# Layer 2's pooled gate from seven block products per pair of tiles, with sums of weights made by DMA

## The chip, the cores and the metric

The kernel runs on one core of a Trainium2 chip. The metric is the device time of one execution, in microseconds; lower is better.

## What is computed

A residual stream of 528 tokens (16 learned ones ahead of 512) and 1024 features goes through two layers. The parts that matter here:

```python
h = rmsnorm(x)                                   # x * rsqrt(mean(x*x) + eps) * gain
u_pool, z_pool, c_q, c_kv, k_rope, z_mla, g_pool, g_mla = split(h @ w_in)
y_pool = (pool_mix(u_pool) * silu(z_pool)) @ pool_w_up
y_mla  = (attention(c_q, c_kv, k_rope) * silu(z_mla)) @ mla_w_up
x = x + (sigmoid(g_pool) * y_pool + sigmoid(g_mla) * y_mla) @ w_out
```

Attention is causal, with 8 heads, and normalises queries and keys. g_pool and g_mla are 1024 features wide each. Only the last 512 tokens of the second layer are put out.

## The kernel before

**Numbers and tiles.** Features lie on the 128 partitions, tokens run along the row. Every fp32 product is made of three matmuls of a faster 32-bit type: activations x and weights w are split into a rounded part and the rest (xh + xl, wh + wl), and mm3 (L184 to L187) accumulates wh*xh, wh*xl and wl*xh in PSUM. Activations of the normalised stream are hs: eight pairs hh, hl of 128 features each. hs holds x times the gain, without the norm's factor inv; what reads a product of hs multiplies by inv (tile rinv) when it empties PSUM. The lines are those of before, which the profile of before carries; in the changed kernel the same lines stand further down.

**The stream.** Weights are read once, in chunks of 128x512 (256 KB). SP loads a chunk into one of three buffers raw; ScalarE rounds it to whi (L180), VectorE subtracts to get wlo (L181), three buffers each. A list called plan holds the products (Gemm) in order: an output tile of 128 features is one Gemm of one or two chunks, whose eviction (evac) runs when its last chunk is through. In layer 1 (the second of two, counted from 0) a tile covers 512 tokens, so a chunk is 12 matmuls of 512 columns and a tile of 1024 inputs is 24. The generator stream() puts out two k steps at a time; clk adds up their planned time. The names in layer 1's plan: pu (pooled path up, into xb), zm (attention's silu gate), gp (pooled gate, eight tiles gp0 to gp7), gm (attention's gate, eight tiles), mu (attention up), o (output).

**Order of the work.** go() writes a layer out. Attention's steps are put between pieces of the stream: fill and gap advance the stream by a planned time (FILL, one number per layer), fill_now by a given one, upto to the end of a named product, after() postpones a function until clk has gone on. A scheduler then settles the order on each engine, and behind() adds a wait on another instruction by hand. qk_stats makes nqs (L685), the negative scale of each query, by Newton steps on VectorE. head() multiplies scores into PSUM tiles S (three banks), finds row maxima on VectorE with nqs (L730), takes exponentials on ScalarE (L737), the reciprocal of their sums on VectorE (L769), and normalises on GpSimd (L774, L776). pv() transposes the result on TensorE (L796), splits it, and multiplies by the values (L801, L802) into one PSUM bank o. Other products use four PSUM banks mm.

**Evictions the change touches.** ev_silu empties zm with two operations on VectorE and one on ScalarE (L505 to L508). ev_gp empties a tile of gp: VectorE multiplies by inv (L573), ScalarE takes tanh, VectorE multiplies into xb (L575). ev_gm: VectorE multiplies by inv (L873), ScalarE takes tanh (L874), and the gate stays in SBUF until ev_mu (L882) reads it. ev_pu writes xb (L567). ev_o adds the residual, loaded from DRAM scratch (scr), and stores (L898). In layer 1, scr holds the stream that came out of layer 0.

## Time and profile before

| | us |
|---|---|
| median of 3 runs | 790.47 (789.48 to 790.82) |
| span of the profiled execution | 787.1 |
| median less that span | 3.4 |
| TensorE busy in it | 780.9 |
| VectorE busy | 535.1 |
| ScalarE busy | 410.8 |
| GpSimd busy | 194.4 |

The profiled execution's own time is its span; what lies around it (start and end of the launch) is the third row, by the median. Engines: PE is TensorE, PEld its weight loads, DVE VectorE, ACT ScalarE, POOL GpSimd, SP the queue that issues most transfers. A row of the time line gives start, duration, engine, line, operation, the tile written and those read, shapes, and in brackets the idle time ahead of it with what ended it. Busy times of engines beside TensorE add up work that lies next to it.

### The profile page before, as it was taken

What the parts mean: (1) busy time and instruction counts of PE and PEld (TensorE: products, weight loads), DVE (VectorE), ACT (ScalarE), POOL (GpSimd) and SP (SyncE); (2) the same over time, 40 slices, a digit from 0 to 9 for tenths busy, and PEclk for the clock granted to TensorE, in tenths of its full rate; (3) what the DMA queues carried; (4) which work ended last, traced back from release to release, by engine and by line L of the source; (5) the groups of instructions that cost most, each with busy time, mean ns of one, the idle gap of its engine ahead of it and who ended that gap; (6) DMA issues with size and microseconds to landing.
All of it is one profiled execution on the core that took longest, in us unless ns stands there. A gap on an engine that the chain in (4) does not pass through costs nothing.

```text
span 787.1 us, 14567 instructions
## 1 busy us (share of the span) xinstructions
PE 780.9 (99%) x5301; PEld 708.6 (90%) x5301; DVE 535.1 (68%) x1165; ACT 410.8 (52%) x930; POOL 194.4 (25%) x259
## 2 busy tenths in 40 slices
PE   9999999999999999999999999999999999999998
PEld 8999899999999999999997898887788888887887
DVE  5848787446779987675464487775467888755932
ACT  7645655635656565633354356455445666554420
POOL 1034504002333242051000145131022333410500
PEclk9999999999999999999999999999999999999999
DMA  6242333423223212224642422334232222122372
GB/s 242 82 102 85 96 120 102 128 81 94 96 76 92 78 58 78 95 81 146 192 123 94 95 88 90 129 88 136 96 105 88 95 84 82 65 81 67 102 242 84
DMA packets 52263, 81.83 MB, mean 104 GB/s; under 512 B 8784, under 2 KB 17360, under 8 KB 52192
## 3 DMA queue, kind: packets, MB, share of 16 engines
q1 hardware_dynamic: 52048, 80.65, 32.9%
q8 instruction: 41, 0.67, 0.4%
q14 instruction: 30, 0.25, 0.1%
q10 hardware_dynamic: 144, 0.26, 0.1%
HBM read 74.49 MB, written 4.27 MB: 100 GB/s over the span
## 4 chain that ended last, share of the span: by engine, by line
PE 95%; DMA 2%; DVE 1%; issue 1%; ACT 0%; SPq 0%; ACTq 0%
PE mm L185 28%; PE mm L187 28%; PE mm L186 28%; PE mm L796 2%; PE S L186 2%; PE S L187 1%; PE S L185 1%; PE o L802 1%; PE o L801 1%; PE S L453 1%; DMA xb<-xT 1%; PE mm L355 1%; DVE wlo L181 1%; PE mm L412 0%; DMA rinv<-win 0%
## 5 line engine op out<-in xcount | busy, mean ns | idle before, releaser
L185 PE MATMUL mm<-hh,whi 128*128 128x264 f32 (+2 forms) x1096 | 346.7, 318 | 0.2 <-ACT racc L810 0.2
L186 PE MATMUL mm<-hl,whi 128*128 128x264 f32 (+2 forms) x1096 | 343.9, 315 | 0.0
L187 PE MATMUL mm<-hh,wlo 128*128 128x264 f32 (+2 forms) x1096 | 343.0, 315 | 0.0
L181 DVE TENSOR_TENSOR wlo<-raw,whi 128x512 fp32r<-128x512 f32 (+2 forms) x251 | 188.6, 755 | 119.6 <-ACT whi L180 115.9
L180 ACT ACTIVATE whi<-raw 128x512 fp32r<-128x512 f32 (+2 forms) x251 | 150.4, 601 | 187.5 <-PE mm L186 126.5
L185 PEld LDWEIGHTS mm<-hh,whi 128*128 128x128 f32 x1096 | 205.9, 188 | 13.6 <-ACT racc L810 0.5
L186 PEld LDWEIGHTS mm<-hl,whi 128*128 128x128 f32 x1096 | 206.6, 189 | 11.8
L187 PEld LDWEIGHTS mm<-hh,wlo 128*128 128x128 f32 x1096 | 205.5, 188 | 12.0
L774 POOL TENSOR_TENSOR pm<-pa,rs 128x16 f32<-128x16 f32 x32 | 11.6, 361 | 181.3 <-DVE rs L769 181.3
L560 POOL TENSOR_TENSOR racc<-racc,tmp 128x264 f32<-128x264 f32 (+1 forms) x15 | 14.2, 948 | 153.8 <-ACT tmp L559 129.8
L702 POOL TENSOR_TENSOR tmp<-kp,bc 64x528 f32<-64x528 f32 x16 | 22.5, 1408 | 76.9 <-PE mm L675 44.5
L884 POOL TENSOR_TENSOR tmp<-tmp,xb 128x264 f32<-128x264 f32 (+1 forms) x24 | 27.1, 1149 | 58.2 <-DVE tmp L882 33.1
L730 DVE CUSTOM_DVE_ANT_0 S<-S,maskw,nqs 128x272 f32<-128x272 f32 (+4 forms) x80 | 38.5, 498 | 4.2 <-PE S L187 3.9
L737 ACT ACTIVATE cq<-S,bia 128x400 f32<-128x400 f32 (+2 forms) x48 | 24.6, 516 | 22.6 <-DVE bia L764 12.0
L185 PE MATMUL mm<-u,whi 128*128 128x264 f32 (+1 forms) x108 | 35.2, 326 | 0.0
L187 PE MATMUL mm<-cq,wlo 128*128 128x264 f32 (+1 forms) x108 | 34.5, 323 | 0.7 <-DVE wlo L181 0.7
L187 PE MATMUL mm<-u,wlo 128*128 128x264 f32 (+1 forms) x108 | 34.8, 323 | 0.0
L185 PE MATMUL mm<-cq,whi 128*128 128x264 f32 (+1 forms) x108 | 34.6, 320 | 0.0
L186 PE MATMUL mm<-cq,whi 128*128 128x264 f32 (+1 forms) x108 | 34.5, 321 | 0.0
L277 DVE TENSOR_TENSOR tl<-mm,th 128x512 fp32r<-128x512 f32 (+1 forms) x64 | 29.3, 481 | 6.1 <-ACT th L276 5.1
L776 POOL TENSOR_TENSOR cq<-cq,rs 128x384 f32<-128x384 f32 (+1 forms) x32 | 32.8, 1025 | 0.0
L186 PE MATMUL mm<-kn,whi 128*128 128x264 f32 (+1 forms) x96 | 30.7, 321 | 0.0
(252 smaller groups left out, 1362.4 us busy)
## 6 DMA issues: line engine op xcount, KB each, us to landing
raw<-win SPq DMA_DIRECT2D x143, 256.0 KB, 2.6
raw<-wout SPq DMA_DIRECT2D x32, 256.0 KB, 2.7
bc<-kdr SPq DMA_DIRECT2D x16, 264.0 KB, 3.6
raw<-wpu SPq DMA_DIRECT2D x16, 256.0 KB, 2.7
raw<-wmu SPq DMA_DIRECT2D x16, 256.0 KB, 2.5
raw<-wqb SPq DMA_DIRECT2D x12, 256.0 KB, 2.6
tmp<-xT SPq DMA_DIRECT2D x16, 132.0 KB, 3.0
tmp<-scr SPq DMA_DIRECT2D x7, 256.0 KB, 3.4
```

The lines of the kernel that those rows point to most:

```text
L180: act.activation(hi[:, :n], raw[:, :n], AF.Copy)
L181: dve.tensor_sub(lo[:, :n], raw[:, :n], hi[:, :n].bitcast(F32))
L185: pe.matmul(out, wh, xh, start=start, stop=False)
L186: pe.matmul(out, wh, xl, start=False, stop=False)
L187: newest[0] = pe.matmul(out, wl, xh, start=False, stop=stop)
L277: dve.tensor_sub(lo[:, a:b], src, hi[:, a:b].bitcast(F32))
L702: gp.tensor_mul(kf[r0:r0 + 64, :], self.kp[r0:r0 + 64, :], bc[r0:r0 + 64, :])
L730: dve.tensor_tensor_reduce(out=sv, in0=sv, in1=mask, scale=nqs[:, i, h:h + 1], scalar=3e38, op0=ALU.add, op1=ALU.min, accum_out=bia[:, c:c ...
L737: act.activation(pv, sv, AF.Exp, scale=-1.0, bias=bia[:, i:i + 1], accum_out=rs[:, c:c + 1])
L776: gp.tensor_mul(pt[i][:, NM:], pt[i][:, NM:], rs[:, i:i + 1].to_broadcast([P, n - NM]))
L796: pe.transpose(tr[:, P * (i - j):P * (i - j + 1)], pt[i][:, NM + P * j:NM + P * (j + 1)], ident)
L884: gp.tensor_add(t[:, :b - a], t[:, :b - a], self.am[m][:, a:b])
```

## The change

**Seven products.** For a pair of gp tiles (2u and 2u + 1), the weights are split in two by output tile and in two by input features, the activations in two by input features and in two by tokens (256 each). A 2x2 product of blocks takes eight block products; fast() takes seven, on sums and differences of blocks, and puts the results together afterwards. A block product is one chunk of weights: 12 matmuls of 256 columns, so a pair is 84, where before it was 48 of 512. The products 1, 2 and 4 use a quarter of the weights as they are, the others a sum from DRAM (wsum). PSUM holds a pair in four banks: 1 and 2 in a, 6 in b, 7 and 4 in c, 5 and 3 in d. ScalarE and VectorE (copy, sub, add of 256 columns) join them; got_gp takes tanh and multiplies into xb. The plan's order is now gm0 gm1 gp0 gm2 gp1 gm3 gp2 gm4 gp3 gm5 gm6 gm7, where gp0 to gp3 are the pairs; before it was gp0 to gp7, then gm0 to gm7.

**Sums of weights.** Four per pair, 16 in all. Each is a copy from DRAM to DRAM (256 KB, on SP) and a DRAM-to-DRAM transfer that adds to it (on GpSimd's queue), postponed one by one by SPACE = 4500 of planned time from the start of layer 0's heads. Each waits for a matmul that lies 9000 or 4000 of planned time back.

**Normalised activations.** In layer 1, during qk_stats, renorm() makes hs again with inv in it (four of the eight from xb, four loaded from scr): eight multiplies and eight splits. mixed() makes the differences of activation blocks and splits them, in pieces between the heads' steps. zm and gm then need no inv: ev_zm and ev_gate begin with tanh on ScalarE, straight from PSUM.

**Room.** gm0 to gm5 are stored to DRAM (gate) and loaded again after gm6, because SBUF holds the new blocks meanwhile; the tables for rotary positions share two buffers with them. FILL of layer 1 goes from 2850 to 2700, and flush() at the heads' end, which ran everything postponed, becomes ready(), which runs what is due within 12000. A matmul of head 0's scores in each layer waits for the newest one of the stream.

```diff
-FILL = (2950.0, 2850.0)
+FILL = (2950.0, 2700.0)
...
+SPACE = 4500.0
...
-    def mm3(out, wh, wl, xh, xl, start, stop):
-        pe.matmul(out, wh, xh, start=start, stop=False)
-        pe.matmul(out, wh, xl, start=False, stop=False)
-        newest[0] = pe.matmul(out, wl, xh, start=False, stop=stop)
+    def mm3(out, wh, wl, xh, xl, start, stop, more=False, hold=False):
+        first = pe.matmul(out, wh, xh, start=start, stop=False, skip_group_check=more)
+        if hold:
+            behind(first, newest[0])
+        pe.matmul(out, wh, xl, start=False, stop=False, skip_group_check=more)
+        newest[0] = pe.matmul(out, wl, xh, start=False, stop=stop, skip_group_check=more)
+        past.append((clk[0], newest[0]))
+
+    past = []
+
+    def earlier(ns):
+        return next((m for c, m in reversed(past) if c <= clk[0] - ns), past[0][1])
...
+    def ready():
+        while pend and pend[0][0] <= clk[0] + 12000.0:
+            pend.pop(0)[1]()
...
+    wsum = [dp.tile([P, 4, 512], F32, name=f"wsum{u}") for u in range(4)]
+    gate = dp.tile([P, 6, SEQ], F32, name="gate")
...
+    N2 = SEQ // 2
+    XH = [(NM, NM + N2), (NM + N2, T)]
+    (a, b), (_, c) = XH
+
+    def weight_sums(w):
+        def made(u, i):
+            a, b = w[2 * u], w[2 * u + 1]
+            d = wsum[u]
+            src = {0: (b[:, 0:512], b[:, 512:1024]), 2: (a[:, 0:512], b[:, 0:512]), 1: (a[:, 0:512], d[:, 0, :]),
+                   3: (a[:, 512:1024], d[:, 1, :])}
+            return d[:, i, :], src[i]
+
+        def copy(d, src):
+            behind(sp.dma_start(d, src[0]), earlier(9000))
+
+        def add(d, src):
+            behind(gp.dma_start(d, src[1], accum_op=ALU.add), earlier(4000))
+
+        for u in range(4):
+            for fn, i in ((copy, 0), (copy, 2), (add, 0), (copy, 1), (add, 2), (add, 1), (copy, 3), (add, 3)):
+                yield lambda fn=fn, u=u, i=i: fn(*made(u, i))
...
+        def ev_zm(self, m):
+            def ev(ps, a, b):
+                if a == self.x0:
+                    self.zms[m] = slot(f"u{m}")
+                t = tmp()
+                act.activation(t[:, :b - a], ps, AF.Tanh, scale=0.5)
+                dve.scalar_tensor_tensor(out=self.zms[m][:, a:b], in0=t[:, :b - a], scalar=1.0, in1=ps,
+                                         op0=ALU.add, op1=ALU.mult)
+            return ev
+
+        def renorm(self, k):
+            assert k < 4 or (self.l, f"pu{k}") not in done
+            f = self.f[k] = slot("sv", bufs=2) if k % 4 == 3 else slot(f"cq{k}")
+            f, (hh, hl), x = f[:, NM:T], self.hs[k], xb[:, k, NM:T]
+            if k < 4:
+                sp.dma_start(f, scr[:, k, :])
+                x = f
+            behind(dve.scalar_tensor_tensor(out=f, in0=x, scalar=self.g(G_H + k), in1=self.inv[:, NM:T],
+                                            op0=ALU.mult, op1=ALU.mult), newest[0])
+            split(hh, hl, f, NM, T)
...
+        def mixed(self, i):
+            k, s = divmod(i, 2)
+            if k > 3 or not self.last:
+                return
+            u, w = self.f[k], self.f[k + 4]
+            if s == 0:
+                dve.tensor_sub(w[:, b:c], u[:, b:c], w[:, b:c])
+                dve.tensor_sub(u[:, b:c], u[:, a:b], u[:, b:c])
+                dve.tensor_sub(u[:, a:b], u[:, a:b], w[:, b:c])
+                dve.tensor_sub(w[:, a:b], w[:, a:b], u[:, a:b])
+                return
+            if k == 0:
+                self.half = [sqt().bitcast(F32R) for _ in range(14)]
+                spare = slot("rinv", F32R)
+                self.half += [spare[:, 0:HALF], spare[:, HALF:T]]
+            th, tl = (slot(f"cq{(3, 0, 1, 2)[k] + j}", F32R) for j in (0, 4))
+            t3h, t3l, t4h, t4l = (t[:, :N2] for t in self.half[4 * k:4 * k + 4])
+            split(th, tl, u[:, a:c], a, c)
+            for h_, l_, v in ((t3h, t3l, w[:, b:c]), (t4h, t4l, w[:, a:b])):
+                split(h_, l_, v, 0, N2)
+            self.tt[k] = {6: (th[:, a:b], tl[:, a:b]), 5: (th[:, b:c], tl[:, b:c]), 7: (t3h, t3l), 4: (t4h, t4l)}
+
+        def fast(self, name, a, b, u, got):
+            order = (1, 6, 7, 5, 2, 4, 3)
+            s = wsum[u]
+            src = {1: a[:, 0:512], 2: a[:, 512:1024], 4: b[:, 512:1024], 5: s[:, 0, :], 6: s[:, 1, :], 7: s[:, 2, :],
+                   3: s[:, 3, :]}
+            bank = {}
+
+            def body(i, w):
+                p = order[i]
+                key = {1: "a", 2: "a", 6: "b", 7: "c", 4: "c", 5: "d", 3: "d"}[p]
+                if key not in bank:
+                    bank[key] = mmt()
+                ps = bank[key][:, :N2]
+                t, o = (XH[1] if p == 3 else XH[0]), (0 if p == 1 else 4)
+                for k in range(4):
+                    xh, xl = (x[:, t[0]:t[1]] for x in self.hs[k + o]) if p < 4 else self.tt[k][p]
+                    c = P * k
+                    mm3(ps, w[0][:, c:c + P], w[1][:, c:c + P], xh, xl, k == 0 and p not in (2, 4, 3), k == 3, True)
+                    if k == 1:
+                        yield 6 * (N2 / 2.4)
+                if p == 1:
+                    self.part[u] = slot("sv", bufs=2)
+                d, v = self.part[u][:, 0:N2], self.part[u][:, HALF:HALF + N2]
+                if p == 1:
+                    act.activation(d, ps, AF.Copy)
+                elif p == 6:
+                    dve.tensor_sub(d, d, ps)
+                elif p == 7:
+                    dve.tensor_sub(v, ps, d)
+                elif p == 5:
+                    dve.tensor_sub(v, v, ps)
+                    got(2 * u + 1, XH[1], v, v)
+                elif p == 2:
+                    got(2 * u, XH[0], ps, tmp()[:, :N2])
+                elif p == 4:
+                    x = tmp()[:, :N2]
+                    dve.tensor_sub(x, ps, d)
+                    got(2 * u + 1, XH[0], x, x)
+                else:
+                    dve.tensor_add(d, d, ps)
+                    got(2 * u, XH[1], d, d)
+                if i == len(order) - 1:
+                    done.add((self.l, name))
+                yield 6 * (N2 / 2.4)
+
+            plan.append(Gemm((self.l, name), [src[p] for p in order], 512 * len(order), body=body))
...
+        def got_gp(self, m, s, v, t):
+            am = self.am[m][:, s[0]:s[1]]
+            act.activation(t, v, AF.Tanh, scale=0.5)
+            dve.scalar_tensor_tensor(out=am, in0=t, scalar=1.0, in1=am, op0=ALU.add, op1=ALU.mult)
...
-            fill_now(9500)
+            if self.last:
+                start = clk[0]
+                for i, k in enumerate((4, 5, 6, 7, 0, 1, 2, 3)):
+                    self.renorm(k)
+                    fill_to(start + 1500 * (i + 1))
+            else:
+                fill_now(9500)
...
+                    hold=hold and i == 1)
...
+            between()
...
+        def ev_gate(self, m):
+            def ev(ps, a, b):
+                self.gms[m] = slot(f"cq{m}" if m > 5 else "ts" if m % 2 else "tc")
+                act.activation(self.gms[m][:, a:b], ps, AF.Tanh, scale=0.5)
+                if m < 6:
+                    act.dma_start(gate[:, m, :], self.gms[m][:, a:b])
+            return ev
+
+        def gates_again(self):
+            for m in range(6):
+                self.gms[m] = slot(f"cq{m}")
+                sp.dma_start(self.gms[m][:, NM:T], gate[:, m, :])
...
-                add(f"zm{m}", wi(MT_ZM + m), D, evac=self.ev_silu(self.zms, "u", m), xs=hs, segs=XS)
-            for m in range(8):
-                add(f"gp{m}", wi(MT_GP + m), D, evac=self.ev_gp(m), xs=hs, segs=XS)
-            for m in range(8):
-                add(f"gm{m}", wi(MT_GM + m), D, evac=self.ev_gm(m), xs=hs, segs=XS)
+                add(f"zm{m}", wi(MT_ZM + m), D, evac=self.ev_zm(m) if self.last else self.ev_silu(self.zms, "u", m),
+                    xs=hs, segs=XS)
+            if self.last:
+                for e in ("gm0", "gm1", "gp0", "gm2", "gp1", "gm3", "gp2", "gm4", "gp3", "gm5", "gm6", "gm7"):
+                    m = int(e[2])
+                    if e[:2] == "gp":
+                        self.fast(e, wi(MT_GP + 2 * m), wi(MT_GP + 2 * m + 1), m, self.got_gp)
+                    else:
+                        add(e, wi(MT_GM + m), D, evac=self.ev_gate(m), xs=hs, segs=XS)
+            else:
+                for m in range(8):
+                    add(f"gp{m}", wi(MT_GP + m), D, evac=self.ev_gp(m), xs=hs, segs=XS)
+                for m in range(8):
+                    add(f"gm{m}", wi(MT_GM + m), D, evac=self.ev_gm(m), xs=hs, segs=XS)
...
-            fill_now(2600)
+            if l == 0:
+                fill_now(2600)
+                for i, fn in enumerate(weight_sums([win[1, MT_GP + m] for m in range(8)])):
+                    after(SPACE * (i + 1), fn)
             kq = self.prep(0)
             fill_now(2600)
             due[0] = None
             prev = None
             for h in range(H):
-                kn_ = self.head(h, kq, prev)
+                kn_ = self.head(h, kq, prev, lambda: self.mixed(next(mix)))
                 self.gap()
+                self.mixed(next(mix))
                 if h + 1 < H:
                     kq = self.prep(h + 1)
                 self.pv(prev, (2, 3))
                 prev = kn_
                 self.gap()
+                self.mixed(next(mix))
             fill_now(1300)
             self.pv(prev, (0, 1))
             fill_now(2600)
             if not self.last:
                 self.meta_queries()
             self.pv(prev, (2, 3))
+            up("gm6")
+            if self.last:
+                self.gates_again()
             up("gm7")
-            flush()
+            ready()
```

**On TensorE**, where the pooled gate is made. Before, six rows of tile gp1 (a PSUM tile mm, rounded and rest of hs, weights whi and wlo):

```order
L185 MATMUL mm_7893<-hh_14_133,whi_7889 128x512
L186 MATMUL mm_7893<-hl_15_134,whi_7889 128x512
L187 MATMUL mm_7893<-hh_14_133,wlo_7890 128x512
L185 MATMUL mm_7893<-hh_16_135,whi_7889 128x512
L186 MATMUL mm_7893<-hl_17_136,whi_7889 128x512
L187 MATMUL mm_7893<-hh_16_135,wlo_7890 128x512
```

After, six rows of a product on the differences (sq holds them), then two of a product on hs itself:

```order
L188 MATMUL mm_8215<-sq_7738,whi_8151 128x256
L191 MATMUL mm_8215<-sq_7739,whi_8151 128x256
L192 MATMUL mm_8215<-sq_7738,wlo_8152 128x256
L188 MATMUL mm_8215<-sq_7742,whi_8151 128x256
L191 MATMUL mm_8215<-sq_7743,whi_8151 128x256
L192 MATMUL mm_8215<-sq_7742,wlo_8152 128x256
L188 MATMUL mm_8134<-hh_14_136,whi_8231 128x256
L191 MATMUL mm_8134<-hl_15_137,whi_8231 128x256
```

The three kinds of matmul stay; each now has 256 columns, and 336 of them stand where 192 were.

**On VectorE**, from the last split of head 0's keys (kl) on. Before, with the weight splits and the first Newton steps (na, ny, nt):

```order
L277 TENSOR_TENSOR kl_7514<-tmp_7508,kh_7513 128x528
L181 TENSOR_TENSOR wlo_7431<-raw_7428,whi_7430 128x512
L181 TENSOR_TENSOR wlo_7451<-raw_7448,whi_7450 128x512
L681 SCALAR_TENSOR_TENSOR na_7380<-mm_7374,eps_6011 128x32
L681 SCALAR_TENSOR_TENSOR na_7380<-mm_7374,eps_6011 16x8
L284 TENSOR_SCALAR ny_7381<-na_7380 128x40
L285 TENSOR_SCALAR ny_7381<-ny_7381 128x40
L286 TENSOR_SCALAR na_7380<-na_7380 128x40
```

After, from the same row, and then the rows up to nqs and to head 0's first row maximum:

```order
L296 TENSOR_TENSOR kl_7580<-tmp_7574,kh_7579 128x528
L184 TENSOR_TENSOR wlo_7480<-raw_7477,whi_7479 128x512
L573 SCALAR_TENSOR_TENSOR cq_1395_7462<-xb,gn,rinv_6066 128x512
L296 TENSOR_TENSOR hl_15_137<-cq_1390_7438,hh_14_136 128x512
L573 SCALAR_TENSOR_TENSOR cq_1396_7473<-xb,gn,rinv_6066 128x512
L296 TENSOR_TENSOR hl_17_139<-cq_1395_7462,hh_16_138 128x512
L184 TENSOR_TENSOR wlo_7509<-raw_7506,whi_7508 128x512
```

```order
L847 TENSOR_TENSOR tmp_7761<-kn_1132_6312,bc_6914 64x528
L184 TENSOR_TENSOR wlo_7783<-raw_7780,whi_7782 128x512
L825 TENSOR_SCALAR nqs_7436<-ny_7418 128x40
L562 SCALAR_TENSOR_TENSOR u_1447_7721<-tmp_7722,mm_7662 128x512
L184 TENSOR_TENSOR wlo_7830<-raw_7827,whi_7829 128x512
L877 ISA S_7618,bia_7616<-S_7618,maskw,nqs_7436 128x272
```

Before, 17 rows stand between kl and nqs; after, 70. What came in between are the multiplies by rinv (into cq and sv), the splits into hl, and the subtractions and splits of mixed.

**On GpSimd**, ahead of layer 0's first head (pm and pa are its softmax blocks). Before:

```order
L702 TENSOR_TENSOR tmp_2696<-kp_967,bc_1522 64x528
L774 TENSOR_TENSOR pm_2643<-pa_2525,rs_2529 128x16
L776 TENSOR_TENSOR pa_2525<-pa_2525,rs_2529 128x128
L774 TENSOR_TENSOR pm_2643<-pa_2525,rs_2529 128x16
L776 TENSOR_TENSOR pa_2525<-pa_2525,rs_2529 128x256
```

After:

```order
L848 TENSOR_TENSOR tmp_2703<-kp_972,bc_1527 64x528
L351 DMA wsum_123<-win 128x512
L922 TENSOR_TENSOR pm_2649<-pa_2530,rs_2534 128x16
L924 TENSOR_TENSOR pa_2530<-pa_2530,rs_2534 128x128
L922 TENSOR_TENSOR pm_2649<-pa_2530,rs_2534 128x16
L924 TENSOR_TENSOR pa_2530<-pa_2530,rs_2534 128x256
```

One transfer that adds to wsum now stands ahead of the normalisation; nine more stand between later heads, two at a time at most, and the last six behind the last head, among the gated sums (L884) of layer 0's mu.

24 lines of the change are left out of this document (17 added, 7 removed).

## The prediction

> **What bounds the kernel now.** I read the page from the top: the busy times, the forty slices, and the chain of work that ended last.
>
> ```profile
> span 787.1 us, 14567 instructions
> ...
> PE 780.9 (99%) x5301; PEld 708.6 (90%) x5301; DVE 535.1 (68%) x1165; ACT 410.8 (52%) x930; POOL 194.4 (25%) x259
> ...
> PE   9999999999999999999999999999999999999998
> ...
> DVE  5848787446779987675464487775467888755932
> ...
> PEclk9999999999999999999999999999999999999999
> ...
> PE 95%; DMA 2%; DVE 1%; issue 1%; ACT 0%; SPq 0%; ACTq 0%
> ```
>
> TensorE is busy in every slice, it has 95% of the chain, and its clock was granted in full. So the span is the sum of the distances from one matmul's start to the next. A matmul taken away is worth its distance, and any other engine counts only where it makes TensorE wait. VectorE is the engine to watch: in layer 1's attention its slices stand at 7 to 8 tenths.
>
> The page's duration of a matmul is longer than its distance, so I take distances from the tail, where nothing disturbs them. The first fence is the time line of VectorE, the second that of TensorE.
>
> ```profile
> 772.61 0.69 DVE L898 SCALAR_TENSOR_TENSOR tmp<-mm,tmp 128x512 f32<-128x512 f32 x1 [1.65 <-PE mm L187]
> ...
> 778.15 0.69 DVE L898 SCALAR_TENSOR_TENSOR tmp<-mm,tmp 128x512 f32<-128x512 f32 x1 [1.65 <-PE mm L187]
> 782.41 0.42 DVE L898 SCALAR_TENSOR_TENSOR tmp<-mm,tmp 128x256 f32<-128x256 f32 x1 [3.57 <-PE mm L187]
> 783.83 0.42 DVE L898 SCALAR_TENSOR_TENSOR tmp<-mm,tmp 128x256 f32<-128x256 f32 x1 [0.99 <-PE mm L187]
> ```
>
> ```profile
> 772.40 0.39 PE L185 MATMUL mm<-hh,whi 128*128 128x512 f32 x1
> 772.64 0.39 PE L186 MATMUL mm<-hl,whi 128*128 128x512 f32 x1
> ```
>
> Each of these evictions waits for the last matmul of a tile. One whole tile, 24 matmuls of 512 columns, takes 778.15 - 772.61 = 5.54 us, **231 ns** a matmul. The last twelve matmuls of 256 columns take 783.83 - 782.41 = 1.42 us, **118.3 ns** each.
>
> **The change part by part.** *Fewer products.* Before, gp0 to gp7 of layer 1 are 8 tiles x 24 = 192 matmuls of 512 columns: 8 x 5.54 = 44.3 us. After, four pairs x 7 products x 12 = 336 matmuls of 256 columns: 28 x 1.42 = 39.8 us. The other matmuls keep their number and shape. The saving is **4.6 us**, if every product runs at the distance of the tail. The products use whole 128x128 weights and 256 contiguous columns, as the rows of the tail do, so I take 118.3. Break-even lies at 44.3 / 336 = 132 ns.
>
> What could speak against this price is the weight load that goes with each matmul:
>
> ```profile
> L185 PEld LDWEIGHTS mm<-hh,whi 128*128 128x128 f32 x1096 | 205.9, 188 | 13.6 <-ACT racc L810 0.5
> ```
>
> A load lasts 188 ns on the mean, more than 118; were it not overlapped, 336 x 188 = 63 us would be 19 us more than before. The tail's twelve matmuls in 1.42 us had their loads too, so it is overlapped. The Trainium skill, "TensorE: Matmul & The Clock Gate", section "Back-to-back issue gap", gives a sustained 81 ns at 128 columns and 131 at 512 for matmuls with their loads; a straight line between them is an estimate of 98 ns at 256, and by it the change would lose 336 x 98 - 192 x 131 = 7.8 us. The trace does not agree: 231 and 118.3 are nearly in the ratio of the columns.
>
> *Work added to VectorE and ScalarE.* Prices come from the groups of layer 1's attention (560 to 720 us; the last two numbers ahead of the second bar are busy us and mean ns), beside the busy times of that part by stretch:
>
> ```profile
> L181 DVE TENSOR_TENSOR wlo<-raw,whi 128x512 fp32r<-128x512 f32 x46 | 35.1, 764 | 15.5 <-ACT whi L180 15.0
> L873 DVE TENSOR_TENSOR cq<-mm,rinv 128x512 f32<-128x512 f32 x8 | 5.5, 690 | 6.2 <-PE mm L187 6.2
> L573 DVE TENSOR_TENSOR tmp<-mm,rinv 128x512 f32<-128x512 f32 x8 | 5.5, 689 | 4.2 <-PE mm L187 4.2
> ...
> L575 DVE SCALAR_TENSOR_TENSOR xb<-tmp,xb 128x512 f32<-128x512 f32 x8 | 5.5, 684 | 0.5 <-ACT tmp L574 0.4
> ...
> L277 DVE TENSOR_TENSOR tl<-mm,th 128x256 fp32r<-128x256 f32 x8 | 3.3, 417 | 2.5 <-ACT th L276 2.3
> L505 DVE SCALAR_TENSOR_TENSOR u<-mm,rinv 128x512 f32<-128x512 f32 x4 | 2.8, 691 | 3.9 <-PE mm L187 3.9
> ```
>
> ```profile
> core 0: us, PE busy (x) PEld busy (x) DVE busy (x) ACT busy (x) POOL busy (x), PEclk, DMA share, GB/s
> 552.00:572.00 20.00, 20.00 (x90) 15.76 (x90) 8.64 (x23) 7.45 (x13) 1.32 (x1) 1.00 0.24 84
> 572.00:594.00 22.00, 22.00 (x110) 18.50 (x109) 14.71 (x35) 10.74 (x26) 6.00 (x9) 1.00 0.30 102
> 594.00:660.00 66.00, 66.00 (x347) 56.12 (x346) 55.96 (x125) 40.46 (x101) 23.75 (x36) 1.00 0.29 89
> 660.00:715.00 55.00, 54.70 (x283) 45.77 (x282) 37.61 (x86) 32.06 (x79) 13.03 (x25) 1.00 0.22 70
> ```
>
> VectorE gains 12 weight splits (28 chunks instead of 16: 9.2 us), 8 multiplies and 8 splits of the renormalisation (16 x 0.69 = 11.0), 16 subtractions and 8 splits of 256 columns and 4 splits of 512 in mixed (24 x 0.417 + 4 x 0.69 = 12.8), and 36 operations of 256 in the pairs' evictions (15.0): 48.0 us. It loses the two groups of gp, that of gm and one of zm's: 5.5 + 5.5 + 5.5 + 2.8 = 19.3. Net **+28.7 us** on the 116.9 of the four stretches, in 163 us less 4.6: from 72% to 92% by durations. ScalarE goes up by some 21 us on 90.7 and stays at 70%. So VectorE has room, but not much by durations. Its starts follow more closely than its durations say:
>
> ```profile
> 609.29 0.68 DVE L573 TENSOR_TENSOR tmp<-mm,rinv 128x512 f32<-128x512 f32 x1
> 609.89 0.68 DVE L181 TENSOR_TENSOR wlo<-raw,whi 128x512 fp32r<-128x512 f32 x1
> ```
>
> With work waiting, an operation of 512 costs 0.60, not 0.69. Priced by starts, the share is near 80%. These are my two ends for the wait below.
>
> *Where VectorE is late first.* The renormalisation and most of mixed are placed ahead of the Newton steps that give nqs, the scale that head 0's softmax needs. The places in the trace before, on VectorE and on TensorE:
>
> ```profile
> 551.89 0.71 DVE L277 TENSOR_TENSOR kl<-tmp,kh 128x528 fp32r<-128x528 f32 x1
> ...
> 561.33 0.18 DVE L685 TENSOR_SCALAR nqs<-ny 128x40 f32<-128x40 f32 x1
> ```
>
> ```profile
> 567.57 0.40 PE L185 MATMUL mm<-hh,whi 128*128 128x512 f32 x1
> ...
> 591.64 0.38 PE L796 MATMUL mm<-cst,pa 128*128 128x128 f32 x2
> ```
>
> I add up the changed order's VectorE rows from kl on, as if nothing else held them. nqs then comes at 582.9 by starts, at 587.8 by durations, not at 561.3; the last reciprocal of head 0 comes at 589.5 or 595.7; GpSimd's first two normalised blocks 1.4 us later, at 590.9 or 597.1. TensorE's rows of the changed order, added up from zm0's first matmul at 567.57, reach the transposes that read them at 593.5 (591.64 before). So it is 2.6 us early by starts and 3.6 us late by durations. The last normalised input of zm0 comes at 569.5 or 572.1, and is wanted at 572.2: in time by both. I take 0.7 us of the 3.6, since VectorE with work queued goes by starts, and keep 0 to 3.6. After head 0 the reciprocals lead TensorE by 8.9 us and more by starts.
>
> *Sums of weights, during layer 0's heads.* 16 copies stand in SP's queue among the weight loads, 16 accumulating transfers in GpSimd's, ten of them among the softmax normalisations and six behind the last. Each waits for a matmul that lies some microseconds back in the plan (9 for a copy, 4 for an accumulating one), and that is past when its queue comes to it, unless the queue runs ahead of the plan. The nearest rows:
>
> ```profile
> 189.09 0.22 POOL L774 TENSOR_TENSOR pm<-pa,rs 128x16 f32<-128x16 f32 x1 [27.99 <-DVE rs L769]
> ...
> 192.33 1.03 POOL L776 TENSOR_TENSOR cq<-cq,rs 128x512 f32<-128x512 f32 x1
> ```
>
> ```profile
> 195.25 0.38 PE L796 MATMUL mm<-cst,pa 128*128 128x128 f32 x2
> ```
>
> ```profile
> raw<-win SPq DMA_DIRECT2D x143, 256.0 KB, 2.6
> ...
> tmp<-scr SPq DMA_DIRECT2D x7, 256.0 KB, 3.4
> ```
>
> Layer 0's first head is normalised at 193.36, 1.9 us ahead of its transposes. At the low end it costs nothing, as GpSimd was idle 28 us before this head; at the high end it holds GpSimd for a whole landing, 2.6 us, just ahead of each of eight heads: 8 x (2.6 - 1.9) = 5.6 us. I take 0, the queue being free between heads. The Trainium skill, "SBUF — State Buffer", section "A bandwidth-pool intuition that's wrong (but worth ruling out)", tells of a GpSimd transfer of 620 ns that took 3100 beside a VectorE copy; with 3.1 us this end would be an estimated 9.6. No row of before shows such a transfer. A weight load that shares the queues with a copy comes later; three buffers hold chunks ahead, so I price that at 0, and at 2.6 us for one load that is late by a whole landing.
>
> *The rest.* The products take a chunk every 1.42 us where a tile took one every 2.77. A chunk's first step on ScalarE is
>
> ```profile
> L180 ACT ACTIVATE whi<-raw 128x512 fp32r<-128x512 f32 x45 | 28.3, 630 | 32.5 <-PE mm L186 19.6 <-issue 7.8 <-ACT pa L737 2.4
> ```
>
> A load of 2.6 us, this step of 0.63 and the split on VectorE (0.69) are 3.9 us, and a round of three buffers lasts 4.3, without the heads' own steps between: in time, with up to 1 us lost. The six reloads of gates (3.4 us each by the row above, all in flight together) lie under the last gm and the first mu tiles: 0, at most 3.4.
>
> **Sum.** 787.1 - 4.6 + 0.7 = 783.2 for the profiled execution. The median of the runs, 790.47, is 3.4 us above that span (the launch around it), so 783.2 + 3.4 = **786.6**.
>
> **The rivals.** *VectorE holds TensorE (slower).* The mechanism is the one at head 0, with dearer operations. The weight splits of 560 to 720 average 764 ns against 685 to 690 for other operations of that size, 11% more. From kl to head 0's reciprocal are 43.8 us by durations; 11% of it is 4.9, so TensorE waits 3.6 + 4.9 = 8.5 us: 790.5 - 4.6 + 8.5 = 794.4. It decides from a wait of 6.2 us, where the result is 0.2% above before. For it speak the 92%; against it that VectorE reached 0.60 in the rows above. With durations alone the wait is 3.6 to 6: 789.5 to 791.9, no difference. *GpSimd's transfers hold layer 0's heads:* 5.6 us, 792.2; for it the 1.9 us of slack, against it the long idle times between heads. *The halves are not half price:* with unhidden weight loads 790.5 + 18.9 = 809.4; the tail speaks against it. By the estimate from the Trainium skill above it would be 798.3. *The products gain nothing because weights arrive late:* 28 chunks each 0.16 us late eat 4.6 us, 790.5; a round of the three buffers has 0.4 us to spare even without the heads' steps, which give more.
>
> **How the numbers follow.** About 0.2%, 1.6 us, is what a measurement of this kernel can tell from no change. Forecast, 785.3 to 788.8: 0.63. VectorE late by over 6.2 us: 0.14; late by 3 to 6: 0.08. GpSimd's transfers: 0.07, mostly slower. Halves at more than 132 ns: 0.02. Weights late: 0.06, mostly the same. Faster 0.64, the same 0.14, slower 0.22. The range starts at 785.3, the whole saving with no wait and the spread of the runs before, and goes to 793.0, through the case of no difference and part of both slower rivals.
>
> **What would show it.** Right: TensorE's busy time falls by about 4.6 us with starts of 0.118 us in the products, its idle time grows by less than 2, nqs stands near 583 and head 0's transposes near 593. Wrong: TensorE idle at head 0 on GpSimd or VectorE for over 3 us; in layer 0, transposes released by GpSimd behind a transfer; waits on wlo inside the products. If layer 0 ends at another time than before, the transfers are the cause.

## The result, and the profile after

The changed kernel takes 788.28 us (median of 7 runs, 787.37 to 788.95), beside 790.82 for the kernel before on the same chip: ratio 0.9969, 95% interval 0.9957 to 0.9980. A second series on another chip gave 788.00 beside 789.62, ratio 0.9980 (0.9972 to 0.9989). So it is faster, by 1.6 to 2.5 us, 0.2 to 0.3%; forecast were 3.9 us. Two executions among the runs below, one of subs_late (2691 us) and one of subs_behind_hl (1536 us), lie far from all others and are in no ratio.

From the page of the changed kernel, span, busy times and chain. (The changed kernel's lines stand further down: mm3 is L188, L191, L192, the weight split L184, a block's split L296, transposes L944, values L949 and L950.)

```profile
span 786.4 us, 15094 instructions
...
PE 778.8 (99%) x5445; PEld 713.4 (91%) x5445; DVE 558.8 (71%) x1229; ACT 427.1 (54%) x974; POOL 210.9 (27%) x275
...
DVE  5848778447788977685355487775897899874932
...
PE 91%; DVE 4%; DMA 2%; issue 1%; ACT 1%; ACTq 0%; DVEq 0%
```

TensorE still has the chain, but VectorE's part of it rose from 1% to 4%. The same four stretches as before, with the same columns:

```profile
552.00:572.00 20.00, 19.57 (x86) 15.07 (x85) 18.84 (x39) 12.79 (x25) 1.52 (x1) 1.00 0.32 100
572.00:594.00 22.00, 21.58 (x100) 17.66 (x99) 20.78 (x57) 13.41 (x33) 0.19 (x1) 1.00 0.34 106
594.00:660.00 66.00, 65.43 (x439) 59.62 (x438) 58.95 (x139) 45.69 (x118) 26.99 (x44) 1.00 0.42 124
660.00:715.00 55.00, 54.59 (x356) 48.96 (x355) 43.85 (x103) 35.55 (x90) 18.51 (x26) 1.00 0.49 147
```

VectorE's busy time went from 116.9 to 142.4 us of 163, and from 8.6 to 18.8 of 20 in the first stretch: the renormalisation fills it to 94%. TensorE now falls short of the whole stretch in all four; before, only in the last.

The price of a product held. TensorE's time line inside one product of the first pair:

```profile
614.97 0.28 PE L191 MATMUL mm<-cq,whi 128*128 128x256 f32 x1
615.09 0.27 PE L192 MATMUL mm<-cq,wlo 128*128 128x256 f32 x1
615.20 0.28 PE L188 MATMUL mm<-cq,whi 128*128 128x256 f32 x1
```

Starts are 0.11 to 0.12 us apart, as in the tail before; the median over the products is 118 ns.

To see where the rest of the 4.6 us went, I took for each matmul the distance to the next start less the price of its size (231 ns for 512 columns, 121 for 264, 118 for 256, and likewise for the others), and summed what is left over. I call it lost time. The sum of the prices fell by 4.7 us. Lost time, in us:

| stretch | before | changed | changed, second profile | whole tiles (an experiment below) |
|---|---|---|---|---|
| 530 to 720, layer 1 from before zm0 to the heads' end | 3.4 | 6.3 | 5.8 | 2.4 |
| of it 560 to 580, zm0 | 0.1 | 1.4 | 1.4 | 0.1 |
| of it 600 to 620, first pair | 0.3 | 1.4 | 1.4 | 0.3 |
| of it 680 to 700, last pair | 0.3 | 1.2 | 0.8 | 0.3 |

So 2.4 to 2.9 us of the 4.7 came back as waits, nearly all at three places; that leaves 1.8 to 2.3, in keeping with the runs. From layer 0's last eviction of o to the kernel's last one, it is 380.0 us before and 378.3 and 377.8 in the two profiles of the changed kernel. Layer 0 itself ended at 403.8 in the one profile of before and at 405.0 and 404.7 in these. That is within what one profile can differ from the next: in the profiles of the experiments below that leave layer 0 as the change made it, it ends between 404.7 and 406.3, and once at 409.2.

The profile of before also lies at the low end. Over the 70 runs of the kernel before that stand beside the experiments, on three chips, the median span is 787.6 to 788.0 us, and that profile's is 787.1; the changed kernel's 18 runs have 786.4 and 786.1. In these runs the time is 1.8 us above the span at the median. So of the 3.4 us that I took for the launch, an estimated 1.6 are the distance of that one profile from the median of its three runs.

**At zm0** TensorE waits for VectorE twice; its time line, then VectorE's:

```profile
570.55 0.40 PE L191 MATMUL mm<-hl,whi 128*128 128x512 f32 x1
571.37 0.50 PE L191 MATMUL mm<-hl,whi 128*128 128x512 f32 x1 [0.43 <-DVE hl L296]
571.71 0.39 PE L192 MATMUL mm<-hh,wlo 128*128 128x512 f32 x1
571.93 0.40 PE L188 MATMUL mm<-hh,whi 128*128 128x512 f32 x1
572.75 0.50 PE L192 MATMUL mm<-hh,wlo 128*128 128x512 f32 x1 [0.42 <-DVE wlo L184]
```

```profile
558.57 1.83 DVE L184 TENSOR_TENSOR wlo<-raw,whi 128x512 fp32r<-128x512 f32 x1
...
569.97 0.41 DVE L583 TENSOR_TENSOR cq<-cq,cq 128x256 f32<-128x256 f32 x1
570.31 0.41 DVE L584 TENSOR_TENSOR cq<-cq 128x256 f32<-128x256 f32 x1
570.64 0.67 DVE L296 TENSOR_TENSOR hl<-cq,hh 128x512 fp32r<-128x512 f32 x1
571.25 0.40 DVE L585 TENSOR_TENSOR cq<-cq,cq 128x256 f32<-128x256 f32 x1
571.58 0.18 DVE L309 SCALAR_TENSOR_TENSOR ny<-nt,ny 128x40 f32<-128x40 f32 x1
571.69 0.41 DVE L583 TENSOR_TENSOR sv<-sv,sv 128x256 f32<-128x256 f32 x1
572.03 0.67 DVE L184 TENSOR_TENSOR wlo<-raw,whi 128x512 fp32r<-128x512 f32 x1
572.63 0.67 DVE L296 TENSOR_TENSOR hl<-sv,hh 128x512 fp32r<-128x512 f32 x1
```

Right ahead of the split hl and of the weight split wlo for which TensorE waits stand subtractions of mixed (L583 to L585), for products that come over 40 us later. And one weight split took 1.83 us, beside a GpSimd operation. The split waited for is the last but one of the renormalisation; the last one is through at 573.30, and TensorE does not wait for it.

**At head 0**, which I had priced, TensorE does not wait: nqs comes at 586.11, the reciprocal at 593.48, the transposes start at 596.25. **At the first pair** TensorE waits for the bank o, which VectorE empties late (TensorE, then VectorE):

```profile
616.84 0.50 PE L949 MATMUL o<-th,vt 128*128 128x512 f32 x1 [0.55 <-DVE tmp L965]
```

```profile
612.96 1.50 DVE L847 TENSOR_TENSOR tmp<-kn,bc 64x528 f32<-64x528 f32 x1
614.49 1.70 DVE L184 TENSOR_TENSOR wlo<-raw,whi 128x512 fp32r<-128x512 f32 x1
616.11 0.67 DVE L965 TENSOR_TENSOR tmp<-o,tmp 64x512 f32<-64x512 f32 x1
```

The two operations ahead of the eviction are over twice as long as their kind is without a GpSimd operation beside it (0.70 and 0.69 us); GpSimd works from 609.98 to 615.63 us. Without these 1.8 us, and in the same order, the eviction would have come before TensorE asked for it.

**At the last pair** TensorE waits for a join that frees a bank (TensorE, then VectorE):

```profile
685.09 0.39 PE L188 MATMUL mm<-sq,whi 128*128 128x256 f32 x1 [0.33 <-DVE sv L625]
```

```profile
683.67 0.68 DVE L184 TENSOR_TENSOR wlo<-raw,whi 128x512 fp32r<-128x512 f32 x1
...
684.63 0.41 DVE L625 TENSOR_TENSOR sv<-sv,mm 128x256 f32<-128x256 f32 x1
```

Here VectorE's operations have their usual length, and GpSimd runs nothing from 677.4 to 687.5 us: the join stands behind a queue of other work.

**In layer 0**, GpSimd's queue ahead of the first head, and the summary of its transfers:

```profile
186.08 0.96 POOL L351 DMA_DIRECT2D wsum<-win  x1 [24.50 <-PE mm L192]
189.66 0.21 POOL L922 TENSOR_TENSOR pm<-pa,rs 128x16 f32<-128x16 f32 x1 [2.62 <-DVE rs L917]
```

```profile
L351 POOL DMA_DIRECT2D wsum<-wsum x8: 787/828/862, 208.4 to 369.6; - x8
...
DMA to landing us min/median/max: 4.3/5.8/7.4
```

A transfer holds GpSimd for 0.8 to 0.96 us and is through 2.6 us before the head needs the engine; landing takes 4.3 to 7.4 us, and nobody waits.

### The profile page after: what moved, and what is told of

The parts are those of the page before. It is cut to its first block, busy times and chain, and to the rows that moved or that the text cites. A ratio compares the mean times of both kernels' runs of the same rounds, so it can differ in the third digit from the quotient of the medians.

```text
span 786.4 us, 15094 instructions
## 1 busy us (share of the span) xinstructions
PE 778.8 (99%) x5445; PEld 713.4 (91%) x5445; DVE 558.8 (71%) x1229; ACT 427.1 (54%) x974; POOL 210.9 (27%) x275
## 4 chain that ended last, share of the span: by engine, by line
PE 91%; DVE 4%; DMA 2%; issue 1%; ACT 1%; ACTq 0%; DVEq 0%
PE mm L188 27%; PE mm L192 27%; PE mm L191 26%; PE mm L944 2%; PE S L191 2%; PE S L192 2%; PE S L188 1%; DVE wlo L184 1%; PE o L950 1%; PE o L949 1%; PE S L498 1%; PE mm L400 1%; DMA xb<-xT 1%; DMA raw<-win 1%; DVE hl L296 0%
## 5 line engine op out<-in xcount | busy, mean ns | idle before, releaser
L188 PE MATMUL mm<-hh,whi 128*128 128x264 f32 (+2 forms) x1080 | 333.9, 311 | 0.1
L191 PE MATMUL mm<-hl,whi 128*128 128x264 f32 (+2 forms) x1080 | 332.5, 309 | 0.4 <-DVE hl L296 0.4
L192 PE MATMUL mm<-hh,wlo 128*128 128x264 f32 (+2 forms) x1080 | 332.1, 310 | 0.4 <-DVE wlo L184 0.4
L184 DVE TENSOR_TENSOR wlo<-raw,whi 128x512 fp32r<-128x512 f32 (+2 forms) x263 | 197.7, 756 | 108.8 <-ACT whi L183 105.3
L183 ACT ACTIVATE whi<-raw 128x512 fp32r<-128x512 f32 (+2 forms) x263 | 157.8, 603 | 179.3 <-PE mm L191 114.6
L188 PEld LDWEIGHTS mm<-hh,whi 128*128 128x128 f32 x1080 | 202.9, 188 | 11.8 <-ACT racc L958 0.5
L191 PEld LDWEIGHTS mm<-hl,whi 128*128 128x128 f32 x1080 | 203.3, 188 | 11.1 <-DVE hl L296 0.9
L192 PEld LDWEIGHTS mm<-hh,wlo 128*128 128x128 f32 x1080 | 202.5, 188 | 10.5 <-DVE wlo L184 1.1
L192 PE MATMUL mm<-cq,wlo 128*128 128x264 f32 (+2 forms) x140 | 43.5, 313 | 0.6 <-DVE wlo L184 0.6
L188 PE MATMUL mm<-cq,whi 128*128 128x264 f32 (+2 forms) x140 | 44.0, 314 | 0.0
L191 PE MATMUL mm<-cq,whi 128*128 128x264 f32 (+2 forms) x140 | 43.4, 311 | 0.0
L877 DVE CUSTOM_DVE_ANT_0 S<-S,maskw,nqs 128x288 f32<-128x288 f32 (+4 forms) x80 | 38.3, 497 | 3.0 <-PE S L192 2.8
L188 PE MATMUL mm<-u,whi 128*128 128x264 f32 (+1 forms) x108 | 35.2, 326 | 0.1
L296 DVE TENSOR_TENSOR tl<-mm,th 128x512 fp32r<-128x512 f32 (+1 forms) x64 | 29.4, 481 | 7.7 <-ACT th L295 6.5
L192 PE MATMUL mm<-u,wlo 128*128 128x264 f32 (+1 forms) x108 | 34.7, 322 | 0.0
L191 PE MATMUL mm<-kn,whi 128*128 128x264 f32 (+1 forms) x96 | 30.6, 320 | 0.0
L188 PE MATMUL mm<-q,whi 128*128 128x264 f32 (+1 forms) x96 | 29.9, 323 | 0.6 <-ACT q L295 0.4
```

The costliest lines, as they stand in the source:

```text
L183: act.activation(hi[:, :n], raw[:, :n], AF.Copy)
L184: dve.tensor_sub(lo[:, :n], raw[:, :n], hi[:, :n].bitcast(F32))
L188: first = pe.matmul(out, wh, xh, start=start, stop=False, skip_group_check=more)
L191: pe.matmul(out, wh, xl, start=False, stop=False, skip_group_check=more)
L192: newest[0] = pe.matmul(out, wl, xh, start=False, stop=stop, skip_group_check=more)
L296: dve.tensor_sub(lo[:, a:b], src, hi[:, a:b].bitcast(F32))
```

## The experiments

My theory after the result: VectorE is late at zm0 and at the pairs, by its amount of work, by its order, or by GpSimd's lengthening it. Rivals: the transfers in layer 0 take part of the gain; the products themselves cost more than TensorE's time.

### The pooled gate in whole tiles again (tiles)

```diff
-                        self.fast(e, wi(MT_GP + 2 * m), wi(MT_GP + 2 * m + 1), m, self.got_gp)
+                        for j in (2 * m, 2 * m + 1):
+                            add(f"gp{j}", wi(MT_GP + j), D, xs=hs, segs=XS,
+                                evac=lambda ps, x, y, j=j: self.got_gp(j, (x, y), ps, tmp()[:, :y - x]))
...
-            if k > 3 or not self.last:
+            if True:
```

> The changed kernel with the pooled gate in eight whole tiles again, without mixed and without the seven products; renormalisation, gates through DRAM, plan order and the transfers of sums stay (the sums are not used). TensorE gets 4.6 us more. If the products' own work on VectorE costs waits (1.1 us near 616, 0.9 near 684), these go, and the waits at zm0 too, since the subtractions are gone: 788.3 + 4.6 - 3 = 790, ratio 0.999 to 1.000. If the waits are those of the renormalisation and of layer 0's transfers, they stay: 788.3 + 4.6 = 793, ratio 1.0025.

Measured: 789.82 us, ratio 1.0007 (0.9998 to 1.0016). The first of the two outcomes. With the seven products go all three waits (last column of the table above), though the renormalisation, the gates through DRAM and the transfers stay. So the seven products and mixed are worth 4.7 us on TensorE and cost 3.4 to 3.9 us of waits; by the runs the net is 1.5 to 3 us (by medians and by ratios), by the profiles about 1. All the other edits together change nothing that can be measured.

### No transfers for the sums (no_sums), and the changed kernel once more (after_again)

```diff
-                for i, fn in enumerate(weight_sums([win[1, MT_GP + m] for m in range(8)])):
-                    after(SPACE * (i + 1), fn)
...
-            src = {1: a[:, 0:512], 2: a[:, 512:1024], 4: b[:, 512:1024], 5: s[:, 0, :], 6: s[:, 1, :], 7: s[:, 2, :],
-                   3: s[:, 3, :]}
+            src = {1: a[:, 0:512], 2: a[:, 512:1024], 4: b[:, 512:1024], 5: b[:, 0:512], 6: a[:, 0:512], 7: b[:, 0:512],
+                   3: a[:, 512:1024]}
```

> The changed kernel without the 32 transfers that make the sums of weights; the products 3, 5, 6 and 7 read blocks of the weights as they are, so the gate is not the reference's. If the transfers hold up layer 0, its end (404.9 us in the profile) comes back to before's 403.8 and the ratio to 0.9955. If the 1.2 us that layer 0 is later are the chip's own spread, the ratio stays at 0.9965 to 0.9975.

> The changed kernel once more, on the chip of subs_back and eight. It serves to set no_sums (0.9981) beside it: if the transfers of sums cost nothing, it gives 0.997 to 0.9985; if they cost 1.2 us, it comes out at 0.9995, with the earlier 0.9969 a spread between chips.

Measured: no_sums 787.93 us, 0.9981 (0.9972 to 0.9989); after_again 788.00, 0.9980 (0.9972 to 0.9989). Layer 0 ends at 404.96 without the transfers and at 404.71 and 404.99 with them. The 32 transfers are free to within the measurement. That all profiles but the one of before have layer 0 ending 0.9 us later or more is then no price of the transfers. It is less than the 1.5 us by which profiles with the same layer 0 differ, and the profile of before lies at the low end, as said above.

### Eight products per pair (eight)

```diff
-            order = (1, 6, 7, 5, 2, 4, 3)
+            order = (1, 6, 7, 5, 2, 4, 2, 3)
...
+                elif p == 2 and i > 4:
+                    pass
                 elif p == 2:
```

> The changed kernel with eight products per pair: product 2 is run twice, so the gate is not the reference's. 48 matmuls of 256 columns, four more weight loads and splits. If each product is paid by TensorE at 118.3 ns a matmul, it adds 48 x 0.1183 = 5.7 us: ratio about 1.004. If the products go slower than that because VectorE or the loads hold them, it adds over 7 us; if other waits hide them, under 4.

Measured: 796.47 us, 1.0096 (1.0081 to 1.0111), 8.5 us above after_again. Four chunks cost 2.1 us each, not 1.42: TensorE's 5.7 us, and lost time up from 5.8 to 8.5 us between 530 and 720. That is the expectation's second case, but not by weight splits alone. Of the waits that are new, one is for a weight split (654 us, 0.6 us); three are for the splits th and tl that the values need (643 and 702 us, 2.1 us together) and one is for a bank S (663 us, 0.4 us). With longer products the heads' steps also fall at other places, so this run does not tell a lack of room on VectorE from another order. The second product 2 goes into a bank that has been read by then, so the gate stays as it was, other than the expectation says.

### The subtractions held back: subs_late, subs_back, subs_behind_hl

One line of mixed, in three ways, and the last of the renormalisation's splits remembered for the third:

```diff
-                dve.tensor_sub(w[:, b:c], u[:, b:c], w[:, b:c])
+                behind(dve.tensor_sub(w[:, b:c], u[:, b:c], w[:, b:c]), newest[0])        # subs_late
+                behind(dve.tensor_sub(w[:, b:c], u[:, b:c], w[:, b:c]), earlier(5000))    # subs_back
+                behind(dve.tensor_sub(w[:, b:c], u[:, b:c], w[:, b:c]), self.ready_hl)    # subs_behind_hl
```

> The changed kernel with the sixteen subtractions of mixed held back: the first of each four waits for the newest matmul of the stream, so that they no longer run ahead of the last splits into hl and of nqs. If VectorE at zm0 is what TensorE waits for there (0.59 + 0.59 us in the profile of the changed kernel), both waits go and nqs comes some 6 us earlier than 586.1: ratio to before about 0.9955, 1.2 us under the changed kernel's 0.9969. If the waits come from late loads, or the subtractions are only missing later, the time stays at 0.997 or rises above it, with new waits at head 1 or at the first products.

> subs_late once more for its profile, the first one having been taken with TensorE at a fraction of its speed. If VectorE stands at the head of its queue behind a matmul that is yet to come, its idle time there is released by TensorE, and TensorE then waits for wlo, hl or nqs for some 4 us in all around heads 0 to 3. If the loss lies at the products, TensorE waits for the differences (cq, sq) there.

> As subs_late, but the first of each four subtractions waits for a matmul that lies 5000 of planned time back, not for the newest one planned, which TensorE reaches only later. If subs_late lost its 4 us because VectorE stood at the head of its queue waiting for a matmul, this one stays clear of that: the waits at zm0 (1.2 us) go, ratio 0.995 to 0.996. If the subtractions do harm anywhere but ahead of nqs, it is slower than the changed kernel here too, 0.999 or more.

> The changed kernel with each of the four groups of subtractions of mixed kept behind the last split into hl of the renormalisation (a wait of VectorE on its own earlier operation), instead of among them. It mends only the two waits at zm0. If these are due to the subtractions standing ahead of the last splits, they go (0.59 + 0.59 us) and nqs stays at 586: ratio 0.9965 if the changed kernel's is 0.998, 1.2 us less. If VectorE's whole amount of work counts, the wait appears again later, and it is 0.998.

Measured: subs_late 1.0033 (1.0020 to 1.0045), subs_back 1.0056 (1.0037 to 1.0075), subs_behind_hl 1.0043 (1.0025 to 1.0061). The profile of subs_late is of a separate single execution of 795.84 us, 3.2 us above the slowest of the five in its ratio. All three do what they were to do at zm0: lost time from 560 to 580 falls from 1.4 to 0.2 or less. So the order is the cause of those two waits: VectorE does the subtractions later, and the scheduler also puts head 0's first scores ahead of the second wait on TensorE. And all three lose 4 to 5 us to the changed kernel, at the heads. In subs_back (the profile is of the fastest of its eight runs), nqs comes at 571.8 instead of 586.1, the subtractions stand among the first heads' row maxima, and TensorE finds no free bank S (waits of TensorE, the longest; then its time line):

```profile
PE S L188 <- ACT cq L884: 1.7, 1, 1.7
```

```profile
611.64 0.27 PE L192 MATMUL S<-kh,qhl 128*128 128x144 f32 x1
613.65 0.39 PE L188 MATMUL S<-kh,qhl 128*128 128x272 f32 x1 [1.74 <-ACT cq L884]
```

In subs_late it is the same kind of wait at 621, a join at 633 and a weight split at 655 us. That VectorE stood idle behind a matmul to come, as I had supposed there, is not the main loss, since subs_back, whose first subtraction waits for a matmul well past, loses as much. In the profile of subs_late, besides, a weight load of layer 0 came 3.6 us late, at a time of the transfers for the sums, and its layer 0 ended 4.2 us later than the changed kernel's; it is the only profile with that, and it accounts for that execution's distance from the five. ScalarE's row:

```profile
333.02 1.15 ACT L183 ACTIVATE whi<-raw 128x512 fp32r<-128x512 f32 x2 [3.56 <-DMA raw<-wmu]
```

In subs_behind_hl the order change reaches as far as 651 us. There the heads' work on VectorE falls beside a whole normalisation on GpSimd (VectorE, then TensorE):

```profile
649.12 2.95 DVE L847 TENSOR_TENSOR tmp<-kn,bc 64x528 f32<-64x528 f32 x1
652.11 2.98 DVE L184 TENSOR_TENSOR wlo<-raw,whi 128x512 fp32r<-128x512 f32 x2
```

```profile
655.14 0.65 PE L192 MATMUL mm<-hh,wlo 128*128 128x512 f32 x1 [3.40 <-DVE wlo L184]
655.58 0.63 PE L188 MATMUL mm<-hh,whi 128*128 128x512 f32 x1
...
658.57 0.48 PE L191 MATMUL mm<-hl,whi 128*128 128x512 f32 x1
658.89 0.40 PE L192 MATMUL mm<-hh,wlo 128*128 128x512 f32 x1
659.12 0.39 PE L188 MATMUL mm<-hh,whi 128*128 128x512 f32 x1
```

This profile is of the slowest of its runs. Of the eleven in the ratio, six took 790.65 to 791.97 us at a mean granted clock of 1.000, and five 794.99 to 797.03 us at 0.996 to 0.998. The granted clock is the share of TensorE's full clock that the profile shows. After the wait of 3.40 us the matmuls start 0.43 us apart instead of 0.23, at a granted clock of 0.57. So in this execution the wait costs 1.6 us beyond its own length; that the other four of the five lose time in the same way is suggested by their clocks, not shown. The six at the full clock still stand 3.4 us above the changed kernel, and none of them was profiled.

### The subtractions left out (no_subs), or on GpSimd (subs_pool)

no_subs takes out the four subtractions of mixed, subs_pool writes them with gp.tensor_sub in place of dve.tensor_sub:

```diff
-                dve.tensor_sub(w[:, b:c], u[:, b:c], w[:, b:c])
-                dve.tensor_sub(u[:, b:c], u[:, a:b], u[:, b:c])
-                dve.tensor_sub(u[:, a:b], u[:, a:b], w[:, b:c])
-                dve.tensor_sub(w[:, a:b], w[:, a:b], u[:, a:b])
```

> The changed kernel without the sixteen subtractions of mixed (the blocks go into the splits as they are, so the gate is not the reference's). VectorE has 6.7 us less, all of it ahead of head 1. If VectorE's amount of work ahead of nqs is what TensorE waits for, the waits at zm0 go, nqs comes 6 us earlier, and the ratio is 0.9965 or less. If the waits at the products (616, 648, 684 us) have their own cause there, these stay, and the gain is 1.2 us at most.

> The changed kernel with the same sixteen subtractions on GpSimd, which is idle there. If VectorE's amount of work in the renormalisation and the first heads costs the 2.8 us that are missing, 6.7 us less of it gives 0.994 to 0.9955. If GpSimd at work makes VectorE's own operations longer, as rows of 1.5 to 1.7 us beside the softmax normalisation suggest, the gain is eaten: 0.997 or more.

Measured: no_subs 791.48 us, 1.0020 (1.0011 to 1.0028); subs_pool 796.75 us, 1.0092 (1.0079 to 1.0106). Both expectations of a gain failed: less work on VectorE does not by itself bring time, since the order changes with it. Without the subtractions nqs comes at 578.3, 8 us earlier, yet zm0 still loses 1.2 us, since the scheduler puts mixed's splits into the place of the subtractions, ahead of the last two hl. VectorE's time line in no_subs:

```profile
569.47 0.68 DVE L296 TENSOR_TENSOR cq<-cq,cq 128x512 fp32r<-128x512 f32 x1
570.08 0.74 DVE L573 SCALAR_TENSOR_TENSOR sv<-sv,gn,rinv 128x512 f32<-128x512 f32 x1
570.74 0.68 DVE L296 TENSOR_TENSOR hl<-cq,hh 128x512 fp32r<-128x512 f32 x1
```

Then the heads run in another order, and the pairs lose 2.7 us from 680 to 700 and 3.1 from 620 to 660, on a weight split and on the joins that free a pair's PSUM bank. The waits of TensorE there:

```profile
PE mm L192 <- DVE wlo L184: 1.5, 2, 0.9
...
PE mm L188 <- DVE sv L634: 0.5, 1, 0.5
PE mm L188 <- DVE sv L625: 0.5, 1, 0.5
PE mm L188 <- DVE sv L621: 0.4, 1, 0.4
```

With the subtractions on GpSimd the renormalisation itself is late: 7.7 us lost from 560 to 600, where the changed kernel loses 1.7. Part of that is the clock again, granted at 0.81 and 0.76 in the two stretches of 4 us from 572 to 580.

### GpSimd's normalisation left out in layer 1 (no_norm)

```diff
-                gp.tensor_mul(pt[i][:, NM:], pt[i][:, NM:],
+                if not self.last:
+                  gp.tensor_mul(pt[i][:, NM:], pt[i][:, NM:],
```

> The changed kernel in which GpSimd leaves out the multiplication of the probabilities by the reciprocals in the second layer (all but the 16 first columns), so that the attention is not the reference's. VectorE's weight splits beside a GpSimd operation take 1.04 us on the mean, others 0.69. If that lengthening is why VectorE is late at 616 and 684 us, those waits go, and the ratio is 0.9965 to 0.9975. If it is the number of VectorE's operations, the waits stay, ratio 0.998.

Measured: 788.33 us, 0.9978 (0.9969 to 0.9986), as the changed kernel. The wait at 616 is gone, and lost time from 600 to 620 is down from 1.4 to 0.4; from 680 to 700 it is 0.5 us, beside 1.2 and 0.8. That fits the expectation's first case but does not show it, since the order changes here too. From 595 us on the heads' steps fall elsewhere on every engine: the eviction of o for which TensorE waited, at 616.11 in the changed kernel, comes at 610.14, and the third head's reciprocal, at 609.73 in the changed kernel, at 617.33. At 616 the cause rests on the rows above, in which two lengthened operations stand ahead of the eviction. At 684 it cannot be the lengthening, as no operation there is lengthened. And from 640 to 680 and from 700 to 720 lost time rises by 0.7 and 0.2 us: TensorE now waits there for a weight split and, at 708 us, for ScalarE. In all, 5.5 us are lost from 530 to 720, beside 5.8 to 6.3.

### More stream ahead of the first pair (plan2850)

```diff
-FILL = (2950.0, 2700.0)
+FILL = (2950.0, 2850.0)
...
-                for e in ("gm0", "gm1", "gp0", "gm2", "gp1", "gm3", "gp2", "gm4", "gp3", "gm5", "gm6", "gm7"):
+                for e in ("gm0", "gm1", "gm2", "gp0", "gm3", "gp1", "gm4", "gp2", "gp3", "gm5", "gm6", "gm7"):
```

> The changed kernel with gm2 ahead of the first pair and the layer's FILL at 2850 as before: between two steps of a head TensorE gets 150 ns of planned time more, so VectorE has more of TensorE's time per head. If VectorE's density in the heads costs the waits at 616 and 684 us, they go: 1 to 1.5 us less, ratio 0.997. If only the order of single rows decides, it is 0.998 with other waits, or above.

Measured: 799.18 us, 1.0113 (1.0097 to 1.0129). Lost time from 530 to 720 is 16.5 us, with waits of up to 2 us on the values, on GpSimd's blocks and on joins, at places where the changed kernel has none:

```profile
PE o L949 <- ACT th L295: 2.9, 2, 1.9
PE mm L944 <- POOL cq L924: 1.3, 1, 1.3
...
PE mm L944 <- DVE tmp L635: 1.1, 1, 1.1
```

After two of its waits the clock is granted at less than the whole here too (0.83 from 646 to 652 us, 0.63 from 688 to 692). The idea that less density helps got no support; where the pairs meet the heads' steps is a likelier reason, which this run does not isolate. No version here beats the changed kernel.

## Why the prediction was right, and where it was off

- **The saving on TensorE** was predicted at 4.6 us and is 4.7 by the sum of the prices. The products run at 118 ns. The two estimates against it, weight loads that are not hidden and the Trainium skill's sustained distances ("TensorE: Matmul & The Clock Gate", section "Back-to-back issue gap"), would have shown as a loss, and did not. This step held. TensorE's busy time on the page fell by only 2.1 us, not by the 4.6 named as a sign: a matmul's duration there (0.39 us at 512 columns) is longer than its distance (0.23) and covers the start of each wait.
- **The wait for VectorE** was the mis-sized term: 0.7 us in the sum, 2.4 to 2.9 in the profiles. The difference, 1.7 to 2.2 us, covers the 1.7 us by which the forecast of 786.6 lies under 788.3. The mechanism was named, the place was wrong. At head 0, where I expected it, nothing waits; kl to nqs takes 32.5 us, where I had 31.0 by starts and 35.9 by durations, so pricing by starts was nearer. At zm0, where I wrote "in time by both", two waits cost 1.3 us. That reading took only the last normalised input, which did come in time. TensorE waited for the one before it and for a weight split, and neither was in the sum; both stand behind subtractions, and in all three runs that hold these back the waits go. The lead was gone by then, for "as if nothing else held them" failed too: between kl and the last split VectorE idled 0.9 us on other engines, and one weight split took 1.1 us longer beside GpSimd.
- **At the pairs** I looked at the reciprocals' lead over TensorE (8.9 us) and did not price the bank o, the joins that free a pair's banks, and GpSimd beside VectorE. The waits at 616 and 684 us come from there: the bank o behind two lengthened operations, and a join behind other work. For the first the lengthening is argued from the rows, for the second the cause beyond the queue stays open.
- **Transfers of sums:** predicted 0, and no_sums says 0. The sign "if layer 0 ends at another time than before, the transfers are the cause" was wrong: it ended later, and it does so without them. The mechanism by which GpSimd would have been held for a landing is refuted: it is held for 0.8 to 0.96 us. The Trainium skill's 3100 ns for a GpSimd transfer beside VectorE ("SBUF — State Buffer", the section named above) was not seen, with VectorE busy 84% of the time that the sixteen held GpSimd; the page's case is beside a copy on VectorE, and VectorE ran none there.
- **The slower rival**, VectorE late by over 6.2 us, did not come true in the changed kernel. Variants in which a few operations are held back or moved came out slower than before (1.003 to 1.009, and 1.011 with another plan). No term of the sum tells their order from the changed kernel's, so that this order was a good one is in part luck.
- **The 3.4 us around the span** are not the launch alone, as the runs' 1.8 us show. It leaves the forecast as it is, which is 790.47 less 3.9, but it means that the span of 783.2 was set against a profile at the low end.

What stays open: why exactly the variants' orders do worse at each head, beyond the waits and the clock named; and the cause of the wait at the last pair.

## What to carry to other kernels

When TensorE has the whole chain, work taken from it is worth its distance between starts only as far as the engine that prepares the operands has time left at that very place: here 4.7 us of matmuls became 1.6 to 2.5 us. In a schedule this full, the order of operations on the preparing engine can outweigh their number: taking sixteen away, which changed the order too, cost 3 us. So an edit to such a schedule is judged by a whole run, and a lead that is computed from sums of durations needs a margin for what a neighbouring engine does to them.
